# A decoder layer's delta rule: keys and queries turned by VectorE and DRAM, gates by Silu, and another column order

## The chip, the cores and the metric

One core of one Trainium2 chip runs the whole layer in one launch. The time is the device time of one execution in microseconds.

## What is computed

```python
h = x + 0.5 * swiglu(rmsnorm(x), w_in1, w_out1)
h = h + hybrid_mixer(rmsnorm(h))
h = h + 0.5 * swiglu(rmsnorm(h), w_in2, w_out2)
y = rmsnorm(h)

# hybrid_mixer(u), 512 tokens of 1024 channels
hq, hf, hi, hg, gq, gk, gv, ga, gb, gz, gate_h, gate_g = split(u @ w_in)
# branch 1 (HGRN2, 8 heads): forget gates from hf, q = silu(hq), values hi,
#   chunked recurrence, rmsnorm, times silu(hg), projection
# branch 2 (gated delta rule, 8 key heads, 16 value heads)
q, k, v = split(silu(causal_short_conv([gq, gk, gv], conv_w)))   # 4 taps
q, k = l2norm(q) * 128 ** -0.5, l2norm(k)
beta, g = sigmoid(gb), -exp(a_log) * softplus(ga + dt_bias)
o = gated_delta_chunked(q, k, v, beta, g)     # triangular solve per chunk, state across chunks
y_g = (rmsnorm(o) * silu(gz)) @ w_branch_gdn
y = sigmoid(gate_h) * y_h + sigmoid(gate_g) * y_g
return y @ w_out
```

All inputs and outputs are float32. The wide products are made of three products of rounded halves (`mm3`).

## The kernel before

The first feed-forward block takes the span up to about 360 us, the mixer up to about 1240, the second feed-forward block the rest. The change lies in the mixer.

The mixer works on *columns*: 128 output channels of one wide product, for 512 tokens. A column is 24 products (8 slices of the input by 3) into one of two PSUM tiles of the tag `mm`, and its weights come as two slabs of 256 KB through SP's DMA queue, which ScalarE and VectorE split into a rounded half and a rest (`maker`, L1819 and L1821). The string `DENSE` gives the order in which `choose` looks for the next column: Q and F are HGRN's queries and forget gates, B its values and output gates, D the two small gates of the delta rule, k, q, v its keys, queries and values, y the first branch's projection, z its output gates. Columns that aren't eligible yet are passed over; the merge gates (`tgate`) fill in where nothing else is.

Every step is a Python generator. The class `Desk` is a planner: a step asks for an engine and names a duration, for a buffer (`get`), for an event (`on`) or for a pause (`lag`), and the planner puts all steps in an order on each engine before anything is built. That order is what the engines run; its durations (`A(512)`, `V(512)`, `LAG`, `EASE` = 2.5) only serve to make it.

The delta rule runs in eight *units* of one key head and two value heads. For a unit u:

- `conv` (L1125 to L1147) empties a k, q or v column's PSUM tile on ScalarE (L1125), makes the first tap on ScalarE (L1132), the other three on VectorE (L1135), a tanh on ScalarE (L1138), and a product on VectorE (L1144 for k and q, L1147 for v), since x(1 + tanh(x/2)) is 2 silu(x). The factors of 2 are undone later. Keys and queries stay with channels on the partitions.
- Values are then turned to have tokens on the partitions: `turn` (L1156, VectorE, 32x32 blocks) and `bounce` (L1162, L1167: a store to DRAM and a load in another order).
- `norms` turns keys and queries by TensorE: four transposes into a PSUM tile of the one bank `e` (L1196). ScalarE copies the keys out (L1199) and sums the squares of both per token (L1203). It starts when the unit before has its masked matrix, event `N`.
- `g_n` makes the coefficients from the key sums (L1220 to L1231; GpSimd takes a power, L1223), the products of keys with keys and queries (L1242, `pgq`, two halves in the bank `e`), masks them, and multiplies them with decays (L1257, L1263).
- `g_e` makes the decays on ScalarE: an absolute difference (L1184) and an Exp (L1187) for each of two heads.
- `g_b` sends the masked matrix through DRAM (L1275, L1281), and GpSimd inverts 32x32 blocks (L1293, L1294); `g_inv` completes the inverse on TensorE, and `g_rec` runs the recurrence over four chunks.
- The outputs are normalised on ScalarE (L1486), turned, and multiplied with the z gate (`gated`). The last unit's are turned by TensorE (L1500) and split at once (L1514).

When all columns are done, `closing` multiplies the 16 heads' outputs with the second branch's projection; its first two columns (d = 0, 1) go head by head. HGRN's query columns end in `h_q`, its output gates in `gate`, the z columns in `zgate`: a tanh on ScalarE and a product on VectorE each.

Of the kernel before, what the change touches and what calls it, by code (L numbers as in the profile page):

```python
# [11 lines left out]
AF = mybir.ActivationFunctionType  # L12
ALU = mybir.AluOpType
# [3 lines left out]
P = 128  # L17
T = 512
NT = T // P
D = 1024  # L20
# [3 lines left out]
EPS = 1e-6  # L24
# [7 lines left out]
LEVELS = (1, 2, 4, 8, 16)  # L32

DENSE = (
# [3 lines left out]
)  # L38
MERGE = (None, None, "a", "a", "b", "b", None, None)
WB = 6  # L40
# [11 lines left out]
FRESH = 5  # L52
LAG = dict(raw=3.5, gb=6.5, nb=6, m=7, out=6.5, back=6, turn=6.5)
EASE = 2.5
LANES = {"a": 2, "b": 2, "d": 1, "e": 1}


# [631 lines left out]
def mixer(tc, mp, e):  # L689
    nc = tc.nc  # L690
    pe, act, dve, pool, sp = nc.tensor, nc.scalar, nc.vector, nc.gpsimd, nc.sync
# [9 lines left out]
    def v3(ap, a):  # L701
        return ap.rearrange("p (a b) -> p a b", a=a)
# [165 lines left out]
    def h_q(i, pt, new):  # L868
        tag = ("fs", "ut")[i % 2]
        if new:  # L870
            yield "get", "ta", 1
            yield *A(512), 1
            th = ta("th")
            act.activation(th, pt, AF.Tanh, scale=0.5)
            yield "get", tag, 1
            yield *V(560), 1
            qq = hq[i] = place(tag, "qq", (P, NT, 192), 4)
            dve.scalar_tensor_tensor(qq[:, :, :P], v3(th, NT), 1.0, v3(pt, NT), op0=ALU.add, op1=ALU.mult)
            D.put("mm")
            D.put("ta")  # L880
            D.fire(("Q", i))
            return
        yield "get", "ta", 2
        yield "on", "rbc"
        yield *V(512), 1
        qs = ta("qs")
        dve.tensor_tensor(qs, pt, rbc, op=ALU.mult)
        D.put("mm")
        yield A(512)
        th = ta("th")  # L890
        act.activation(th, qs, AF.Tanh, scale=0.5)
        yield "get", tag, 1
        yield V(512)
        qq = hq[i] = place(tag, "qq", (P, NT, 192), 4)
        dve.scalar_tensor_tensor(qq[:, :, :P], v3(th, NT), 1.0, v3(qs, NT), op0=ALU.add, op1=ALU.mult)
        D.put("ta", 2)
        D.fire(("Q", i))

    def h_f(i, pt, new):
# [33 lines left out]
    def h_head(i):  # L933
# [7 lines left out]
        q4 = qp.rearrange("p (c g b) -> p c g b", c=NT, b=2)  # L941
# [11 lines left out]
        at = place("on", "ah", (P, NT, P), 8)  # L953
# [28 lines left out]
        for li, hh in enumerate((1, 2, 4, 8, 16, 32, 64)):  # L982
# [37 lines left out]
            tag = ("x", "we")[i % 2] if hh == 1 else ("w", "ft")[i % 2] if hh == 2 else "tm"  # L1020
# [11 lines left out]
        fe, v, g = fl, hv_[i // 2], hg_[i // 2]  # L1032
# [9 lines left out]
        kn = place(tag_n, "hkn", (P, NT - 1, P), 4)  # L1042
# [5 lines left out]
        for c in range(NT):  # L1048
# [4 lines left out]
            o = po[:, c * P:(c + 1) * P]  # L1053
# [28 lines left out]
            act.activation(on[:, c], po[:, c * P:(c + 1) * P], AF.Square, accum_out=ss[:, c:c + 1])  # L1082

        yield V(4)
        dve.tensor_scalar(rho, ss, 4.0 / P, 4.0 * EPS * 4.0 * P, op0=ALU.mult, op1=ALU.add)
        yield "lag", EASE
        yield "use", "POOL", 1.2
        pool.tensor_tensor(rho, rho, mhalf[:, :NT], op=ALU.pow)
# [10 lines left out]
        pt = ps("pt")  # L1099
# [20 lines left out]
    def conv(k, i, pt, out, n):  # L1120

        yield "get", "ta", 2
        yield *A(512), 1
        ci = ta("ci", (P, T + 32))[:, :T + 3]
        act.copy(ci[:, 3:], pt)  # L1125
        D.put("mm")
        yield V(4)
        dve.memset(ci[:, :3], 0.0)
        wc = [cs[:, C_CV + 4 * i + j:C_CV + 4 * i + j + 1] for j in range(4)]
        yield A(512)  # L1130
        y = ta("cy")
        act.activation(y, ci[:, :T], AF.Copy, scale=wc[0])  # L1132
        for j in range(1, 4):
            yield V(550)
            dve.scalar_tensor_tensor(y, ci[:, j:j + T], wc[j], y, op0=ALU.mult, op1=ALU.add)  # L1135
        yield A(512)
        th = ci[:, :T]
        act.activation(th, y, AF.Tanh, scale=0.5)  # L1138
        a, b = (v3(th, n), v3(y, n)) if n else (th, y)
        if k[0] in "qk" and k[1] > 3:  # L1140
            yield "on", ("K", k[1] - 4)
        yield V(512)
        if n:
            dve.scalar_tensor_tensor(out, a, 1.0, b, op0=ALU.add, op1=ALU.mult)  # L1144
            D.put("ta", 2)
        else:
            dve.scalar_tensor_tensor(y, a, 1.0, b, op0=ALU.add, op1=ALU.mult)  # L1147
            yield V(512)
            turn(th, y)
            D.put("ta")  # L1150
            yield from bounce(f"vn{i}", th, out, "ta")
        D.fire(k)

    def turn(out, x):

        dve.transpose(out.rearrange("p (f c j) -> p f c j", f=4, c=NT), x.rearrange("p (c i f) -> p f c i", c=NT, f=4))  # L1156

    def bounce(name, x, out, tag=None):

        yield S  # L1160
        scr = dr.tile([P, T], F32, name=name)
        sp.dma_start(scr, x)  # L1162
        yield "lag", LAG["turn"]
        if tag:
            D.put(tag)
        yield S
        sp.dma_start(out.rearrange("p (r a) -> p r a", r=4), scr.rearrange("(r i) (f a) -> (i f) r a", r=4, f=4))  # L1167
        yield "lag", LAG["turn"]

    def g_e(u, st):  # L1170

        yield "on", "decays", *([("at", 2 * u + 1)] if u < 2 else ["more"]), *([("R", u - 4)] if u > 3 else []), \
            *([("E", u - 1)] if u else [])
        for i in range(2):
            hd_ = 2 * u + i
            yield "get", "gb", 1
            yield "use", "ACT", .1
            gb = places["gb"]("gb", (P, NT, P))
            act.dma_start(gb, gtd[hd_:hd_ + 1].rearrange("o (c b) -> o c b", c=NT).to_broadcast([P, NT, P]))
            yield "lag", LAG["gb"]  # L1180
            a = G["at"][u % 4 * 2 + i]
            for c in range(NT):
                yield A(200)
                act.activation(a[:, c], gb[:, c], AF.Abs, bias=gam[:, c, hd_:hd_ + 1], scale=-1.0)  # L1184
            D.put("gb")
            yield A(512)
            act.activation(a, a, AF.Exp, scale=-1.0)  # L1187
        D.fire(("E", u))

    def norms(u, i, kq, kn, sm):  # L1190
        yield "on", ("kq"[i], u)
        yield "get", "e", 1
        yield T_(Patient(.5))
        pt = ps("ptk", "e")
        for c in range(NT):
            pe.transpose(pt[:, c * P:(c + 1) * P], kq[:, c, i], ident)  # L1196
        if i == 0:
            yield A(512)
            act.copy(kn, v3(pt, NT))  # L1199
        for c in range(NT):  # L1200
            yield A(300)
            pc = pt[:, c * P:(c + 1) * P]
            act.activation(pc, pc, AF.Square, accum_out=sm[:, 0, 4 * i + c:4 * i + c + 1])  # L1203
        D.put("e")
        D.fire(("norm", u, i))

    def g_n(u, st):
# [9 lines left out]
        hs = slice(2 * u, 2 * u + 2)  # L1217
        rk = sm[:, 1, 0:4]
        yield V(4)
        dve.tensor_scalar(rk, sm[:, 0, 0:4], 4.0 * EPS, None, op0=ALU.add)  # L1220
# [10 lines left out]
        dve.tensor_scalar(c2, c2, 0.5, None, op0=ALU.mult)  # L1231
        D.fire(("C", u))
        yield "on", ("q", u)
        yield "on", ("qm", 0), ("n2", u % 2)
# [145 lines left out]
    def g_rec(u, st):  # L1380
# [34 lines left out]
        for c in range(NT):  # L1415
# [36 lines left out]
            if c < NT - 1:  # L1452
# [5 lines left out]
                else:  # L1458
                    for i in range(2):
# [12 lines left out]
        dve.tensor_scalar(sm[:, 7, 0:4], sm[:, 0, 4:8], 4.0 * P * EPS, 16.0 * P * EPS * EPS, op0=ALU.mult, op1=ALU.add)  # L1472
        dve.scalar_tensor_tensor(v3(rho, 2), v3(ss, 2), 4.0 / P, sm[:, 7:8, 0:4].to_broadcast([P, 2, 4]),
                                 op0=ALU.mult, op1=ALU.add)
        yield "lag", EASE
        yield "use", "POOL", 1.4
# [79 lines left out]
    def zgate(i, pt):  # L1556

        g = G["gz"][i // 2 % 3].rearrange("p c b -> p (c b)")[:, i % 2 * T:i % 2 * T + T]
        yield *A(512), 1
        act.activation(g, pt, AF.Tanh, scale=0.5)  # L1560
        yield *V(560), 1
        dve.scalar_tensor_tensor(g, g, 1.0, pt, op0=ALU.add, op1=ALU.mult)
        D.put("mm")
        D.fire(("z", i))

# [7 lines left out]

    def gate(key, g, t, o):

        yield "get", "thg", 1
        yield A(300)
        th = places["thg"]("thg", (P, 256))
        act.activation(th, o, AF.Tanh, scale=0.5)
        yield V(256)  # L1580
        dve.scalar_tensor_tensor(g[:, t], th, 1.0, o, op0=ALU.add, op1=ALU.mult)
        D.put("thg")
        D.put("mm")
        if t == 3:
            D.fire(key)
# [465 lines left out]
```

## Time and profile before

| | |
|---|---|
| median of 3 runs | 1600.07 us (1598.64 to 1600.56) |
| profiled execution | 1599.18 us, span 1597.3 us |
| TensorE, VectorE, ScalarE, GpSimd busy | 1582.3, 1140.7, 847.6, 415.9 us |
| DMA | 220.63 MB, 138 GB/s in the mean |
| granted TensorE clock | 0.998 |

Busy time is the union of an engine's instructions; TensorE's instructions overlap, so 99% busy does not mean that the array is at its peak. In the rows below, L190 to L192 are the three products of `mm3`. A row of a group ends with the busy time, the mean duration in ns, and the idle time of the engine just before with what ended it. A row of the timeline begins with the start and the duration in us.

### The profile page before, as it was taken

The page shows a single profiled execution, that of the slowest core. Times are in us where ns is not written, and L with a number is a line of the kernel's source. Part 1 is how long each engine was busy: PE and PEld are TensorE (multiplying, and loading weights), DVE is VectorE, ACT ScalarE, POOL GpSimd, SP SyncE. Part 2 cuts the span into 40 slices and gives each one's busy share as a digit, 9 for nine tenths or more (in the row PEclk, how much of TensorE's full clock was granted, in tenths as well). Part 3 has the DMA queues.
Part 4 walks back from the last instruction along what each step waited for, and adds up shares of the span by engine and source line. Part 5 has one row for each costly group of instructions (what it writes and reads, how often), then busy time and mean ns, then how long its engine had stood idle before and what let it go on. Part 6 is the DMA issues. An engine that isn't in the chain of part 4 may idle for free.

```text
span 1597.3 us, 29111 instructions
## 1 busy us (share of the span) xinstructions
PE 1582.3 (99%) x10552; PEld 1374.3 (86%) x10552; DVE 1140.7 (71%) x2220; ACT 847.6 (53%) x1912; POOL 415.9 (26%) x725
## 2 busy tenths in 40 slices
PE   9999999999999999999999999999999999999997
PEld 8899998888888888888878888888788899999887
DVE  6988785448858769746788988875545788879333
ACT  5756674334434344645766666565324666667222
POOL 0211212000312222065725676700001221121001
PEclk9999999999999999999999999999999999999999
DMA  5776873333213213555345535557543687685333
GB/s 181 173 161 157 178 169 98 117 119 108 79 55 93 61 47 110 147 159 151 114 141 157 164 120 181 180 189 220 167 128 125 148 183 159 157 184 143 93 90 118
DMA packets 141984, 220.63 MB, mean 138 GB/s; under 512 B 22144, under 2 KB 43392, under 8 KB 141840
## 3 DMA queue, kind: packets, MB, share of 16 engines
q1 hardware_dynamic: 124848, 188.14, 38.8%
q0 software_dynamic: 14400, 26.22, 10.6%
q10 hardware_dynamic: 2592, 4.42, 1.0%
q8 instruction: 83, 1.36, 0.4%
q14 instruction: 61, 0.50, 0.1%
HBM read 195.88 MB, written 22.84 MB: 137 GB/s over the span
## 4 chain that ended last, share of the span: by engine, by line
PE 90%; DMA 3%; issue 3%; DVE 1%; ACT 1%; SPq 0%; POOL 0%; POOLq 0%; ACTq 0%; DVEq 0%
PE pmm L190 19%; PE pmm L191 19%; PE pmm L192 19%; PE px L192 6%; PE px L191 6%; PE px L190 6%; PE pnat L190 2%; PE pnat L192 2%; PE pnat L191 2%; DMA wlo<-w1b 1%; DMA wlo<-w1a 1%; PE pgq L1242 1%; PE pog L1450 1%; PE pw L1434 1%; PE pl L1005 1%
## 5 line engine op out<-in xcount | busy, mean ns | idle before, releaser
L190 PE MATMUL pmm<-uh,whi 128*128 128x512 f32 x879 | 360.1, 410 | 1.4 <-ACT ci L1125 1.4
L192 PE MATMUL pmm<-uh,wlo 128*128 128x512 f32 x879 | 342.9, 390 | 0.0
L191 PE MATMUL pmm<-ul,whi 128*128 128x512 f32 x879 | 342.3, 389 | 0.5 <-DVE ul L1606 0.3
L192 PE MATMUL px<-xs,wlo 128*128 128x256 f32 x1008 | 285.8, 284 | 1.2 <-DMA wlo<-w1b 0.5
L191 PE MATMUL px<-xs,whi 128*128 128x256 f32 x1008 | 285.3, 283 | 0.0
L190 PE MATMUL px<-xs,whi 128*128 128x256 f32 x1008 | 285.3, 283 | 0.0
L1819 ACT CAST whi<-raw 128x512 fp32r<-128x512 f32 x226 | 140.1, 621 | 221.0 <-PE pmm L191 185.7
L1821 DVE TENSOR_TENSOR wlo<-raw,whi 128x512 fp32r<-128x512 f32 x226 | 160.6, 712 | 116.2 <-ACT whi L1819 113.9
L192 PEld LDWEIGHTS pmm<-uh,wlo 128*128 128x128 f32 x879 | 165.1, 188 | 35.8
L192 PEld LDWEIGHTS px<-xs,wlo 128*128 128x128 f32 x1008 | 193.5, 192 | 1.9 <-DMA wlo<-w1b 0.7
L190 PEld LDWEIGHTS pmm<-uh,whi 128*128 128x128 f32 x879 | 165.6, 188 | 34.0 <-ACT ci L1125 2.0
L190 PEld LDWEIGHTS px<-xs,whi 128*128 128x128 f32 x1008 | 193.5, 192 | 0.1
L191 PEld LDWEIGHTS px<-xs,whi 128*128 128x128 f32 x1008 | 193.5, 192 | 0.1
L191 PEld LDWEIGHTS pmm<-ul,whi 128*128 128x128 f32 x879 | 165.7, 189 | 31.0 <-DVE ul L1606 0.6
L330 ACT CAST whi<-sw 128x512 fp32r<-128x512 f32 x144 | 87.6, 613 | 92.8 <-DVE sw L367 72.9
L309 DVE TENSOR_TENSOR wlo<-raw,whi 128x512 fp32r<-128x512 f32 x100 | 77.7, 788 | 76.6 <-ACT whi L330 76.2
L330 ACT CAST whi<-raw 128x512 fp32r<-128x512 f32 x104 | 61.4, 592 | 127.2 <-PE pmm L191 92.0
L228 POOL TENSOR_TENSOR acc<-acc,sqt 128x512 f32<-128x512 f32 x18 | 23.4, 1301 | 310.6 <-ACT sqt L226 310.6
L309 DVE TENSOR_TENSOR wlo<-sw,whi 128x512 fp32r<-128x512 f32 x144 | 98.1, 682 | 0.0
L330 ACT CAST whi<-rw 128x512 fp32r<-128x512 f32 (+1 forms) x130 | 79.6, 613 | 26.1 <-PE px L191 14.0
L190 PE MATMUL pmm<-xs,whi 128*128 128x512 f32 (+1 forms) x238 | 89.8, 377 | 0.0
L191 PE MATMUL pmm<-xs,whi 128*128 128x512 f32 (+1 forms) x238 | 89.8, 377 | 0.0
(480 smaller groups left out, 3211.5 us busy)
## 6 DMA issues: line engine op xcount, KB each, us to landing
raw<-wt SPq DMA_DIRECT2D x160, 256.0 KB
rw<-w1b SPq DMA_DIRECT2D x80, 256.0 KB
rw<-w1a SPq DMA_DIRECT2D x74, 256.0 KB
wlo<-w1b POOLq DMA_DIRECT2D x53, 256.0 KB, 4.9
wlo<-w1a POOLq DMA_DIRECT2D x47, 256.0 KB, 4.9
raw<-w2b SPq DMA_DIRECT2D x41, 256.0 KB
raw<-w2a SPq DMA_DIRECT2D x36, 256.0 KB
raw<-wn SPq DMA_DIRECT2D x32, 256.0 KB
```

The source lines that it names most:

```text
L190: pe.matmul(pt, ah, bh, start=first, stop=False)
L191: pe.matmul(pt, ah, bl, start=False, stop=False)
L192: pe.matmul(pt, al, bh, start=False, stop=last)
L228: add.tensor_tensor(acc, acc, s, op=ALU.add)
L309: dve.tensor_tensor(lo, x, hi.bitcast(F32), op=ALU.subtract)
L330: act.copy(hi, x)
L1005: pe.matmul(pl_[s0:s0 + 32, c * 16:(c + 1) * 16], ke[:, c * P + s0:c * P + s0 + 32], qv[:, c, r, :, 1], start=True, stop=True)
L1242: pe.matmul(pq[:, (c % 2) * 256:(c % 2) * 256 + 256], kq[:, c, 0], kq[:, c].rearrange("p a b -> p (a b)"), start=True, stop=True)
L1434: pe.matmul(pw[:, hd2[i]], ut[:, 4 * i + c], xs[i], start=True, stop=True)
L1450: pe.matmul(po[:, 256 + i * P:256 + (i + 1) * P], at[i][:, c], w[:, hd2[i]], start=True, stop=True)
L1819: act.copy(hi, raw)
L1821: dve.tensor_tensor(lo, raw, hi.bitcast(F32), op=ALU.subtract)
```

## The change

1. `norms` turns keys and queries as the values are turned: `turn` on VectorE, a store to DRAM and a load (`bounce`). ScalarE then copies the keys and sums the squares from SBUF. Four transposes on TensorE and the PSUM tile go, for each key and each query column.
2. Silu is one operation on ScalarE in `conv`, `h_q`, `gate` and `zgate`, in place of tanh and a product on VectorE; the factors of 2 and 4 in the norms' constants go with it.
3. The first conv tap is on VectorE.
4. In `g_e` the two Exps of a unit stand side by side, booked at 4.0 us.
5. `DENSE` has another order.

```diff
 DENSE = (
-    "F0 Q0 F1 Q1 F2 Q2 F3 Q3 D0 B0 B1 F4 Q4 F5 Q5 B2 F6 Q6 F7 Q7 B3 "
-    "k0 q0 k1 q1 y0 y1 y2 y3 v0 v1 y4 y5 y6 y7 k2 q2 v2 v3 z0 z1 k3 q3 v4 v5 z2 z3 k4 q4 v6 v7 z4 z5 "
-    "k5 q5 v8 v9 z6 z7 k6 q6 v10 v11 z8 z9 k7 q7 v12 v13 z10 z11 v14 v15 z12 z13 z14 z15 "
+    "F0 Q0 Q1 F1 F2 Q2 F3 Q3 D0 B0 F4 B1 Q4 Q5 B2 F5 F6 Q6 F7 Q7 B3 k0 q0 k1 q1 y0 y1 y2 y3 v0 v1 y4 y5 "
+    "y6 y7 k2 q2 v2 v3 k3 v4 q3 z0 z1 v5 q4 k4 z2 z3 v6 v7 z4 z5 v8 k5 q5 v9 z6 k6 q6 z7 v10 v11 z8 k7 "
+    "z9 v12 q7 z10 z11 v13 v14 z12 z13 z14 z15 v15 "
 )
...
+TURNED = (0, 1)
...
     def h_q(i, pt, new):
...
-            th = ta("th")
-            act.activation(th, pt, AF.Tanh, scale=0.5)
...
-            dve.scalar_tensor_tensor(qq[:, :, :P], v3(th, NT), 1.0, v3(pt, NT), op0=ALU.add, op1=ALU.mult)
+            act.activation(qq[:, :, :P], v3(pt, NT), AF.Silu)
...
     def conv(k, i, pt, out, n):
...
-        yield A(512)
+        yield V(512)
         y = ta("cy")
-        act.activation(y, ci[:, :T], AF.Copy, scale=wc[0])
+        dve.tensor_scalar(y, ci[:, :T], wc[0], None, op0=ALU.mult)
...
-        yield A(512)
-        th = ci[:, :T]
-        act.activation(th, y, AF.Tanh, scale=0.5)
...
-        yield V(512)
+        yield A(512)
         if n:
-            dve.scalar_tensor_tensor(out, a, 1.0, b, op0=ALU.add, op1=ALU.mult)
+            act.activation(out, v3(y, n), AF.Silu)
             D.put("ta", 2)
         else:
-            dve.scalar_tensor_tensor(y, a, 1.0, b, op0=ALU.add, op1=ALU.mult)
+            act.activation(y, y, AF.Silu)
...
     def g_e(u, st):
...
-            yield A(512)
+        yield "use", "ACT", 4.0
+        for i in range(2):
+            a = G["at"][u % 4 * 2 + i]
             act.activation(a, a, AF.Exp, scale=-1.0)
...
     def norms(u, i, kq, kn, sm):
         yield "on", ("kq"[i], u)
+        if i in TURNED:
+            yield "get", "ta", 1
+            yield V(900)
+            x = ta("kt")
+            turn(x, kq[:, :, i])
+            yield from bounce(f"{'kq'[i]}n{u}", x, x)
+            x4 = x.rearrange("p (r c j) -> p c r j", r=4, c=NT)
+            if i == 0:
+                yield A(512)
+                act.copy(kn.rearrange("p c (r j) -> p c r j", r=4), x4)
+                D.fire(("kc", u))
+            for c in range(NT):
+                yield A(300)
+                act.activation(x4[:, c], x4[:, c], AF.Square, accum_out=sm[:, 0, 4 * i + c:4 * i + c + 1])
+            D.put("ta")
+            D.fire(("norm", u, i))
+            return
         yield "get", "e", 1
...
     def zgate(i, pt):
...
-        act.activation(g, pt, AF.Tanh, scale=0.5)
-        yield *V(560), 1
-        dve.scalar_tensor_tensor(g, g, 1.0, pt, op0=ALU.add, op1=ALU.mult)
+        act.activation(g, pt, AF.Silu)
...
     def gate(key, g, t, o):
...
-        act.activation(th, o, AF.Tanh, scale=0.5)
-        yield V(256)
-        dve.scalar_tensor_tensor(g[:, t], th, 1.0, o, op0=ALU.add, op1=ALU.mult)
-        D.put("thg")
+        act.activation(g[:, t], o, AF.Silu)
```

More of the change, by code (lines that the diff above doesn't have):

```diff
@@ L870, in h_q @@
         if new:
-            yield "get", "ta", 1
+            yield "get", tag, 1
             yield *A(512), 1
-            th = ta("th")
-            act.activation(th, pt, AF.Tanh, scale=0.5)
-            yield "get", tag, 1
-            yield *V(560), 1
             qq = hq[i] = place(tag, "qq", (P, NT, 192), 4)
-            dve.scalar_tensor_tensor(qq[:, :, :P], v3(th, NT), 1.0, v3(pt, NT), op0=ALU.add, op1=ALU.mult)
+            act.activation(qq[:, :, :P], v3(pt, NT), AF.Silu)
             D.put("mm")
-            D.put("ta")
             D.fire(("Q", i))
             return
-        yield "get", "ta", 2
+        yield "get", "ta", 1
         yield "on", "rbc"
@@ L888, in h_q @@
         D.put("mm")
+        yield "get", tag, 1
         yield A(512)
-        th = ta("th")
-        act.activation(th, qs, AF.Tanh, scale=0.5)
-        yield "get", tag, 1
-        yield V(512)
         qq = hq[i] = place(tag, "qq", (P, NT, 192), 4)
-        dve.scalar_tensor_tensor(qq[:, :, :P], v3(th, NT), 1.0, v3(qs, NT), op0=ALU.add, op1=ALU.mult)
-        D.put("ta", 2)
+        act.activation(qq[:, :, :P], v3(qs, NT), AF.Silu)
+        D.put("ta")
         D.fire(("Q", i))
@@ L1084, in h_head @@
         yield V(4)
-        dve.tensor_scalar(rho, ss, 4.0 / P, 4.0 * EPS * 4.0 * P, op0=ALU.mult, op1=ALU.add)
+        dve.tensor_scalar(rho, ss, 1.0 / P, EPS * P, op0=ALU.mult, op1=ALU.add)
         yield "lag", EASE
@@ L1135, in conv @@
             dve.scalar_tensor_tensor(y, ci[:, j:j + T], wc[j], y, op0=ALU.mult, op1=ALU.add)
-        yield A(512)
-        th = ci[:, :T]
-        act.activation(th, y, AF.Tanh, scale=0.5)
-        a, b = (v3(th, n), v3(y, n)) if n else (th, y)
         if k[0] in "qk" and k[1] > 3:
             yield "on", ("K", k[1] - 4)
-        yield V(512)
+        yield A(512)
         if n:
-            dve.scalar_tensor_tensor(out, a, 1.0, b, op0=ALU.add, op1=ALU.mult)
+            act.activation(out, v3(y, n), AF.Silu)
             D.put("ta", 2)
         else:
-            dve.scalar_tensor_tensor(y, a, 1.0, b, op0=ALU.add, op1=ALU.mult)
+            act.activation(y, y, AF.Silu)
             yield V(512)
+            th = ci[:, :T]
             turn(th, y)
@@ L1154, in turn @@
     def turn(out, x):
-        dve.transpose(out.rearrange("p (f c j) -> p f c j", f=4, c=NT), x.rearrange("p (c i f) -> p f c i", c=NT, f=4))
+        dve.transpose(out.rearrange("p (f c j) -> p f c j", f=4, c=NT), v3(x, NT).rearrange("p c (i f) -> p f c i", f=4) if len(x.shape) < 3 else
+                      x.rearrange("p c (i f) -> p f c i", f=4))
     def bounce(name, x, out, tag=None):
@@ L1191, in norms @@
         yield "on", ("kq"[i], u)
+        if i in TURNED:
+            yield "get", "ta", 1
+            yield V(900)
[10 more added lines that the diff above has]
+                act.activation(x4[:, c], x4[:, c], AF.Square, accum_out=sm[:, 0, 4 * i + c:4 * i + c + 1])
+            D.put("ta")
+            D.fire(("norm", u, i))
+            return
         yield "get", "e", 1
@@ L1219, in g_n @@
         yield V(4)
-        dve.tensor_scalar(rk, sm[:, 0, 0:4], 4.0 * EPS, None, op0=ALU.add)
+        dve.tensor_scalar(rk, sm[:, 0, 0:4], EPS, None, op0=ALU.add)
         yield "lag", EASE
@@ L1230, in g_n @@
         dve.tensor_tensor(c1, c3, eg[:, :, hs], op=ALU.mult)
-        dve.tensor_scalar(c2, c2, 0.5, None, op0=ALU.mult)
         D.fire(("C", u))
@@ L1471, in g_rec @@
         yield "use", "DVE", .4
-        dve.tensor_scalar(sm[:, 7, 0:4], sm[:, 0, 4:8], 4.0 * P * EPS, 16.0 * P * EPS * EPS, op0=ALU.mult, op1=ALU.add)
-        dve.scalar_tensor_tensor(v3(rho, 2), v3(ss, 2), 4.0 / P, sm[:, 7:8, 0:4].to_broadcast([P, 2, 4]),
+        dve.tensor_scalar(sm[:, 7, 0:4], sm[:, 0, 4:8], P * EPS, P * EPS * EPS, op0=ALU.mult, op1=ALU.add)
+        dve.scalar_tensor_tensor(v3(rho, 2), v3(ss, 2), 1.0 / P, sm[:, 7:8, 0:4].to_broadcast([P, 2, 4]),
                                  op0=ALU.mult, op1=ALU.add)
@@ L1559, in zgate @@
         yield *A(512), 1
-        act.activation(g, pt, AF.Tanh, scale=0.5)
-        yield *V(560), 1
-        dve.scalar_tensor_tensor(g, g, 1.0, pt, op0=ALU.add, op1=ALU.mult)
+        act.activation(g, pt, AF.Silu)
         D.put("mm")
@@ L1574, in gate @@
     def gate(key, g, t, o):
-        yield "get", "thg", 1
         yield A(300)
-        th = places["thg"]("thg", (P, 256))
-        act.activation(th, o, AF.Tanh, scale=0.5)
-        yield V(256)
-        dve.scalar_tensor_tensor(g[:, t], th, 1.0, o, op0=ALU.add, op1=ALU.mult)
-        D.put("thg")
+        act.activation(g[:, t], o, AF.Silu)
         D.put("mm")
```

## The prediction

> **What bounds the kernel now.** I read the page's busy times and its chain first.
>
> ```profile
> span 1597.3 us, 29111 instructions
> ...
> PE 1582.3 (99%) x10552; PEld 1374.3 (86%) x10552; DVE 1140.7 (71%) x2220; ACT 847.6 (53%) x1912; POOL 415.9 (26%) x725
> ...
> PE 90%; DMA 3%; issue 3%; DVE 1%; ACT 1%; SPq 0%; POOL 0%; POOLq 0%; ACTq 0%; DVEq 0%
> ```
>
> TensorE is busy for 1582.3 of 1597.3 us and makes 90% of the chain that ended last. So an edit saves time only if it takes instructions off TensorE or removes a wait of TensorE, and it costs time only if TensorE has to wait. The profiled execution took 1599.18 us: 1.9 more than its span and 0.9 less than the median of 1600.07. I sum against 1599.18 and add 0.9 at the end.
>
> Next, TensorE's waits that lie in the mixer (from the list of waits), and the busy times by stretch; the mixer's head loop, delta rule and branch products lie from 364 to 1124 us.
>
> ```profile
> PE pmm L190 <- ACT ci L1125: 1.4, 1, 1.4
> ...
> PE pgq L1242 <- ACT ptk L1203: 0.6, 1, 0.6
> ...
> PE pmm L191 <- DVE ul L1514: 0.2, 1, 0.2
> ```
>
> ```profile
> 800.00:900.00 100.00, 98.55 (x629) 80.66 (x628) 87.52 (x187) 67.41 (x192) 53.11 (x112) 1.00 0.49 149
> ...
> 364.00:1124.00 760.00, 756.35 (x5387) 624.19 (x5385) 584.36 (x1313) 417.67 (x1130) 287.25 (x582) 1.00 0.43 131
> ```
>
> In 760 us TensorE is idle for 3.65. The first wait is for ScalarE to empty a column's PSUM tile, the second for ScalarE's squares of the turned keys and queries, the third for the last head's output. VectorE is busy for 87.5 of 100 us in the delta rule, ScalarE for 67.4. Neither is the bound, but VectorE has the smaller margin. The granted clock is 1.00 throughout.
>
> **Part 1: what TensorE loses.** Sixteen sets (keys and queries of eight units) of four transposes go.
>
> ```profile
> L1196 PE MATMUL ptk<-sq,h 128*128 128x128 f32 x48 | 7.3, 274 | 0.0
> ...
> L1196 PE MATMUL ptk<-sq,x 128*128 128x128 f32 x16 | 2.5, 280 | 0.0
> ```
>
> ```profile
> 673.10 0.60 PE L1196 MATMUL ptk<-sq,h 128*128 128x128 f32 x4
> 673.45 0.48 PE L190 MATMUL pmm<-oh,whi 128*128 128x512 f32 x1
> 673.77 0.40 PE L191 MATMUL pmm<-oh,whi 128*128 128x512 f32 x1
> 674.00 0.40 PE L192 MATMUL pmm<-oh,wlo 128*128 128x512 f32 x1
> ```
>
> The groups show 48 + 16 transposes with 9.8 us of busy time, but busy times of neighbours overlap. What counts is the step from start to start. In the timeline a set holds TensorE from 673.10 to 673.45, that is 0.35 us, and the next product takes 0.32 to its successor where the one after takes 0.23: another 0.09 for the change of kind. A set costs 0.35 us where other short products already stand beside it (they make the change of kind anyway) and 0.44 where it stands alone: 5.6 to 7.0 us for sixteen. Most stand alone, so I take **6.8**. The pgq wait of 0.6 goes too, because the bank it waits for no longer holds turned keys: **0.6**. It could be replaced by another wait of that size, so its bounds are 0 and 0.6.
>
> A rule speaks against this part: the Trainium skill's page "VectorE: DVE Perf Modes", section "Rules for kernel authors", advises TensorE for a 128x128 transpose whose destination may be PSUM, and a crossbar DMA otherwise. By that rule the transposes would stay and 6.8 us would not be saved. The trace speaks against the rule here only in that TensorE is the full engine; no run shows the alternative.
>
> **Part 2: what the other engines get.** On VectorE come sixteen turns and 32 first taps; the product after each gate's tanh goes.
>
> ```profile
> L1156 DVE STREAM_TRANSPOSE ci<-cy 128x512 f32<-128x512 f32 x16 | 17.5, 1096 | 0.2
> ...
> L1144 DVE SCALAR_TENSOR_TENSOR h<-ci,cy 128x512 f32<-128x512 f32 x12 | 8.8, 732 | 1.6 <-ACT ci L1138 1.5
> ...
> L1562 DVE SCALAR_TENSOR_TENSOR ggz<-ggz,pmm 128x512 f32<-128x512 f32 x12 | 8.1, 678 | 0.0
> ...
> L922 DVE TENSOR_SCALAR ke<-fs,cf 128x512 f32<-128x512 f32 x8 | 4.9, 615 | 0.1
> ```
>
> Added: 16 x 1.10 + 32 x 0.62 = 37.4 us. Removed: 32 conv products at 0.73, 16 z and 8 query products at 0.68, and 16 half-size ones that I bound by 0.34 to 0.68: 23.4 + 16.3 + 5.4 to 10.9 = 45 to 51. VectorE gains 8 to 13 us in all, but not in the delta rule: if 26 of the 32 conv columns fall there, it gets the 16 turns (17.6) and 26 taps (16.1) and loses 26 conv products (19.0) and 16 z products (10.8), so its load stays within 4 us of what it is. Off TensorE's path: zero, as long as its order holds.
>
> ScalarE loses 32 taps and gets changes of its function table, since Silu and Exp alternate.
>
> ```profile
> L1132 ACT ACTIVATE cy<-ci,cs 128x512 f32<-128x512 f32 x32 | 22.9, 720 | 7.7 <-DVE ci L1128 5.0 <-issue 1.8 <-ACT ci L1125 0.6
> ...
> L1187 ACT ACTIVATE gat<-gat 128x512 f32<-128x512 f32 x8 | 5.1, 632 | 0.2
> ...
> L1579 ACT ACT_TABLE_LOAD x1 | 1.3, 1283 | 0.0
> L482 ACT ACT_TABLE_LOAD x1 | 1.3, 1283 | 0.0
> ```
>
> ```profile
> 357.38 0.62 ACT L563 ACTIVATE rbc<-h 128x512 f32<-128x512 f32 x1
> 358.02 1.28 ACT L736 ACT_TABLE_LOAD   x1
> ```
>
> Between the load at L1579 (tanh) and that at L482 (Silu, second FFN) no load stands, though Exp, tanh and squares alternate: those share a table, Silu is in another. With both Exps of a unit side by side, each of eight units costs two loads: 16 x 1.28 = 20.5 us, against 32 x 0.72 = 23.0 for the taps. ScalarE's sum is unchanged. What is new is a block of 2 x 1.28 + 2 x 0.63 = 3.8 us; the planner books 4.0. Behind it are queued the eviction of a finished column and the weights' casts. A column is 24 products of 0.23 us, 5.5 us, and there are two PSUM tiles, so a block of 3.8 still fits. Cost taken: zero; bounds: the ci wait of 1.4 gone, or one more of it per unit, 8 x 1.4 = 11. I take 0.7 of gain, half of that wait, since the tap that stood between on ScalarE leaves it.
>
> Whether tanh, which the forget gates and merge gates keep, is in Silu's table too no row shows; L1579's load for tanh comes after Ln, not Silu. If it isn't, some 25 tanh among the Silus cost up to 50 more loads. The planner books none, so I take the shared table and keep the other as a rival.
>
> **Part 3: the keys' new way.** The same trip is made today by the values:
>
> ```profile
> 669.61 1.09 DVE L1156 STREAM_TRANSPOSE ci<-cy 128x512 f32<-128x512 f32 x1
> ...
> 670.73 0.34 SPq L1162 DMA_DIRECT2D vn<-ci  x1
> ...
> 678.67 0.43 SPq L1167 DMA_DIRECT2D gvb<-vn  x1
> ...
> 686.79 0.69 DVE L1301 TENSOR_TENSOR gvb<-gvb,sm 128x512 f32<-128x512 f32 x1 [2.71 <-DMA gvb<-vn]
> ```
>
> From the turn's start to the first use, which did wait for the DMA, are 17.2 us, where the transposes cost under one. Each unit's chain (key norm, coefficients, key product pgq, masked matrix, trip through DRAM, GpSimd's inversion) is that much longer, once per unit, and a unit's norms start only when the unit before has its masked matrix. SP gets 32 issues at about 0.4 us (12.8 us over 400), in order with the weights' loads. What does the longer chain delay?
>
> ```profile
> 821.61 0.16 DVE L1220 TENSOR_SCALAR sm<-sm 128x4 f32<-128x4 f32 x1
> 836.88 1.02 PE L1242 MATMUL pgq<-h 128*128 128x256 f32 x4
> 848.45 1.62 DVE L1257 SCALAR_TENSOR_TENSOR gn<-gm,sm,gat 128x128 f32<-128x128 f32 x4
> 855.09 0.76 DVE L1263 TENSOR_TENSOR gat<-gqm,gat 128x512 f32<-128x512 f32 x1
> ...
> 860.37 0.20 POOL L1294 TENSOR_TENSOR gft<-gft,fm 128x8 f32<-128x8 f32 x1
> 873.75 0.25 POOL L1293 TENSOR_TENSOR fm<-gfs,gln 128x31 f32<-128x31 f32 x1 [7.22 <-DMA gln<-hmask]
> ```
>
> ```profile
> L1294 POOL TENSOR_TENSOR gln<-gln,fm x155: 203/327/875, 725.8 to 1036.0; 128x60 f32<-128x60 f32 x15, 128x28 f32<-128x28 f32 x10, 128x54 f32<-128x54 f32 x10, 128x48 f32<-128x48 f32 x10
> ```
>
> For unit 4 the key sums are ready at 821.61 and pgq starts only at 836.88, because the query's transposes and squares sit in the one bank that pgq needs. That delay of 15.3 us disappears. The sums now come some 16.5 us later, at 838; coefficients take about 7 by the planner's figures (two pauses of 2.5, 1.2, 0.8), so pgq is at 845, its two halves take about 6 in a free bank, and the masked matrix starts at 851 instead of 848.45. GpSimd's inversions run from 725.8 to 1036.0 for seven units, 44.3 us each, with 13 us of waiting before unit 4's. A unit's front part in the new way is 17.2 + 2.6 (copy, squares) + 7 + 6 + 7.4 (848.45 to 855.85) = 40 us: under 44.3, so it doesn't become the cadence. Each unit starts 5 us earlier to 3 later.
>
> The end of the delta rule:
>
> ```profile
> 1111.87 0.40 ACT L1486 ACTIVATE on<-x,sm 128x128 f32<-128x128 f32 x1
> ...
> 1116.77 0.60 PE L1500 MATMUL pto<-sq,on 128*128 128x128 f32 x4
> ...
> 1123.39 0.69 DVE L1514 TENSOR_TENSOR ul<-on,uh 128x512 fp32r<-128x512 f32 x1 [0.74 <-ACT uh L1512]
> ```
>
> TensorE just meets the last head today (a wait of 0.2 on L1514). The outputs were ready at 1112.27 and their transposes stood behind columns until 1116.77: 4.5 us of slack. If TensorE arrives 8.1 us earlier and the last head at the same time, 3.6 us of it are waited out. With a last head that is 5 earlier nothing is, with one 3 later 6.6. I take **2.0**. The new column order is not priced: it moves k3 up by two columns of 5.5 us, k4, k6 and k7 by one, and k5 back by one, which on the whole helps these chains.
>
> **Sum.** 1599.2 - 6.8 - 0.6 - 0.7 + 2.0 = 1593.1; with 0.9, **1594.0**. Own range 1589 to 1598. A measurement of this kernel can tell about 0.2% (3.2 us) from no change.
>
> **Rivals.**
> - *The last head eats it* (0.14). The last head comes 3 to 5 us later, and TensorE waits 6 to 8 us before the last products: 1598 to 1600. For it: today's coincidence at 1123. Against: the 4.5 us of slack.
> - *The DRAM trip becomes the cadence* (0.19), the slower side. If the front part takes more than 44.3 us, as with the present 11.6 from pgq to the mask step instead of 6 (45.6), or with SP's queue holding each DMA for a further 2, the excess adds up over the last five units. At 47 us: 5 x 2.7 = 13.5 late, less 4.5 of slack, on top of the saving that is waited out too: 1599.2 + 13.5 - 4.5 + 0.9 = 1609.
> - *ScalarE's block stops the evictions* (0.05). If ScalarE lost as much again at each switch as the load takes, a unit's block would be 3.8 + 2.6 = 6.4 us, 0.9 over the 5.5 of a column: 8 x 0.9 = 7 us of waits, 1601. Against it, the load at 358.02 starts 0.02 after the end of the instruction ahead. The Trainium skill's "ScalarE: Activation LUTs", section "What ACT_TABLE_LOAD costs", states such a loss: 1283 ns for the load and about 1380 for a drain. The trace agrees on the first and shows no drain.
> - *Tanh is not in Silu's table* (0.05): 50 loads, 64 us more on ScalarE; at one column's wait in four, 12 x 1.4 = 17 us: 1610.
>
> **Numbers.** The forecast has 0.57, of which 0.02 are within 0.2%; the first rival 0.14, of which 0.02 are faster; the second 0.19; the third 0.05, within 0.2%; the fourth 0.05. Faster 0.57, same 0.02 + 0.12 + 0.05 = 0.19, slower 0.24. The range 1587 to 1606 leaves out the worst of the slower cases, and below it only what a better column order might add to 8.1 us.
>
> **What would show it.** Right: no ptk rows on TensorE, 64 fewer short products in 364 to 1124, that stretch some 6 us shorter, 16 to 20 table loads of 1.28 us, inversions still about 44 us apart. Wrong: TensorE waits on L1514 or on ci of several us, GpSimd's inversions 46 us apart or more, over 40 table loads.

## The result, and the profile after

| | before | after |
|---|---|---|
| median, 6 runs each on one chip | 1599.65 us | 1619.2 us (1615.88 to 1623.83) |
| ratio, 95% interval | | 1.0127 [1.0113, 1.0142] |
| profiled execution, span | 1599.18, 1597.3 us | 1617.28, 1615.5 us |
| DMA | 220.63 MB | 229.01 MB |

The change costs about 20 us where 6 less were forecast. The page of the kernel after:

```profile
span 1615.5 us, 28996 instructions
...
PE 1583.6 (98%) x10488; PEld 1370.2 (85%) x10488; DVE 1128.5 (70%) x2188; ACT 846.5 (52%) x1899; POOL 407.9 (25%) x725
...
PE 81%; DMA 7%; issue 5%; DVE 4%; ACT 2%; POOL 0%; SPq 0%; POOLq 0%; DVEq 0%; ACTq 0%
```

TensorE has its 64 transposes fewer (10488 for 10552), and VectorE, ScalarE and GpSimd are all less busy than before. Yet TensorE's busy time rose by 1.3 us, and its share of the chain that ended last fell from 90 to 81%; DMAs have 7% of it instead of 3. So nothing was loaded more: something waits. (The chain's shares don't show that by themselves: `pe_turn` below has 83% for TensorE and 6% for DMAs and loses nothing.) The list of TensorE's waits in the mixer (us in total, times, longest) and the busy times of stretches:

```profile
PE pks L1430 <- DVE s L1466: 4.9, 1, 4.9
PE pog L1457 <- DVE ci L1121: 4.0, 1, 4.0
PE pw L1443 <- DVE x L1434: 1.6, 1, 1.6
PE pmm L191 <- ACT ci L1118: 1.6, 2, 0.9
PE pmm L191 <- ACT uh L1521: 1.5, 1, 1.5
PE pmm L191 <- ACT yh L1577: 1.5, 1, 1.5
```

```profile
364.00:1142.00 778.00, 757.62 (x5335) 620.85 (x5334) 572.54 (x1281) 418.70 (x1120) 278.96 (x582) 0.99 0.45 139
...
880.00:888.00 8.00, 6.93 (x33) 5.44 (x31) 1.48 (x6) 4.58 (x15) 2.04 (x8) 1.00 0.99 284
...
835.20:839.20 4.00, 4.00 (x13) 3.33 (x14) 2.85 (x5) 1.88 (x12) 0.00 (x0) 0.57 0.86 261
...
892.00:897.00 5.00, 5.00 (x13) 3.92 (x14) 3.78 (x8) 1.40 (x4) 4.31 (x9) 0.52 0.69 218
897.00:910.00 13.00, 13.00 (x67) 11.04 (x66) 9.20 (x23) 8.37 (x30) 8.33 (x19) 1.00 0.54 160
```

The mixer's stretch is 18 us longer, and TensorE is idle in it for 20.4 us instead of 3.65. The two longest waits are for VectorE, in the recurrence (for `pog` the row names L1121, the last that VectorE had done; what `pog` reads is `gwe`, which VectorE made just before). What held VectorE is in its groups (line, form, count, busy time, mean ns, idle time before and what ended it):

```profile
L1125 DVE TENSOR_SCALAR cy<-ci,cs 128x512 f32<-128x512 f32 x32 | 15.6, 487 | 26.4 <-DMA vn<-ci 13.0 <-DMA od<-zo 6.2 <-DMA td<-tg 3.7
```

The first tap, now on VectorE, is cheap (0.487 us), but five of the 32 wait 22.9 us in all for *stores*: of turned values (`vn<-ci`), of gated outputs (`od<-zo`), of a merge gate (`td<-tg`). The tap reads none of these. It writes `cy`, a buffer of the tag `ta`, and that buffer was last read by the store. The chain that ended last shows one case link by link:

```profile
880.17 7.71 DMA od<-zo
887.98 0.49 DVE cy L1125
...
890.74 0.75 DVE cy L1128
891.88 1.22 PE pks L1430 x2
```

A store issued at 880.17 lands at 887.9, in a stretch with the DMA engines at 0.99; only then the tap has its buffer. Behind it on VectorE stands the copy of the state (L1466) that TensorE's `pks` needs, so TensorE stops for 4.9 us. The 4.0 us wait at 835 has the same history: VectorE's tap stood for 5.64 us until a store of turned values, issued at 823.64, had landed at 829.43. After both waits the clock is low: in 892 to 897 it is 0.52, against 1.00 from 897 on, and in the 4 us after 835 it is 0.57. The products of those 5 us are about 0.43 us apart instead of 0.23, some 2 us more for each long wait. A third such stretch lies at the mixer's end (a clock of 0.50 in 1143 to 1145, after waits of 1.0 and 1.5 us). That is most of why busy time rose with fewer instructions. The Trainium skill's "TensorE: Matmul & The Clock Gate", section "Part 1: The HAM clock gate (the 'warmup' mystery)", says that TensorE falls to half rate after an idle window of about 3.4 us. For the two long waits the trace agrees; the runs also show half rate after less. In `slots8` below, products slow to 0.43 us apart from 709.8 on (clock 0.50 in 710 to 712) after a wait of 1.4 us that ended at 708.26, and not after the wait of 2.1 us that ended at 881.99.

The tag has six buffers. Before, its tiles were held for a column's taps or for a store. Now a turned key's or query's buffer `kt` is held from the turn through both DMAs and the squares. The third unit in the timeline, whose key was turned at 687.84:

```profile
688.98 0.38 SPq L1153 DMA_DIRECT2D kn<-kt  x1
...
697.92 0.42 SPq L1158 DMA_DIRECT2D kt<-kn  x1
...
706.12 0.62 ACT L1194 COPY gkn<-kt 128x512 f32<-128x512 f32 x1 [4.05 <-DMA kt<-kn]
```

From the store's issue to the first use are 17.1 us, and ScalarE stands 4.05 us for the load. From the turn's start it is 18.3 us, the longest of the eight units; the others take 15.2 to 17.7. The buffer is free only after the last square, so it is held longer still. When the tap stands from 881.7 to 887.9, two of the six buffers hold the sixth unit's key and query:

```profile
868.51 1.08 DVE L1146 STREAM_TRANSPOSE kt<-h 128x512 f32<-128x512 f32 x1
...
872.28 1.10 DVE L1146 STREAM_TRANSPOSE kt<-h 128x512 f32<-128x512 f32 x1
...
879.64 0.59 ACT L1118 COPY ci<-pmm 128x512 f32<-128x512 f32 x1
...
880.91 0.58 ACT L1118 COPY ci<-pmm 128x512 f32<-128x512 f32 x1
...
900.98 0.29 ACT L1198 ACTIVATE kt<-kt 128x128 f32<-128x128 f32 x1
```

The last of their squares runs at 900.98. Two buffers hold columns that were just emptied (`ci`), one the turned values whose store was issued at 881.39, and one the gated output whose store lands at 887.9. That makes six.

### The profile page after: what moved, and what is told of

Read it like the earlier page. It is cut to its first block, busy times and chain, and to the rows that moved or that the text cites. A ratio compares the mean times of both kernels' runs of the same rounds, so it can differ in the third digit from the quotient of the medians.

```text
span 1615.5 us, 28996 instructions
## 1 busy us (share of the span) xinstructions
PE 1583.6 (98%) x10488; PEld 1370.2 (85%) x10488; DVE 1128.5 (70%) x2188; ACT 846.5 (52%) x1899; POOL 407.9 (25%) x725
## 2 busy tenths in 40 slices
DMA packets 152735, 229.01 MB, mean 142 GB/s; under 512 B 22656, under 2 KB 52096, under 8 KB 152592
## 4 chain that ended last, share of the span: by engine, by line
PE 81%; DMA 7%; issue 5%; DVE 4%; ACT 2%; POOL 0%; SPq 0%; POOLq 0%; DVEq 0%; ACTq 0%
PE pmm L191 18%; PE pmm L192 17%; PE pmm L193 17%; PE px L193 5%; PE px L192 5%; PE px L191 5%; DMA wlo<-w1b 2%; DMA wlo<-w1a 2%; PE pnat L191 2%; PE pnat L193 2%; PE pnat L192 2%; DMA vn<-ci 1%; PE pgq L1251 1%; PE pog L1459 1%; PE pw L1443 1%
## 5 line engine op out<-in xcount | busy, mean ns | idle before, releaser
L191 PE MATMUL pmm<-uh,whi 128*128 128x512 f32 x879 | 363.8, 414 | 4.7 <-ACT uh L1521 1.5
```

The source lines that it names most:

```text
L191: pe.matmul(pt, ah, bh, start=first, stop=False)
```

## The experiments

Main theory (S): the longer trip holds buffers of `ta`, the taps wait for them, and TensorE behind the taps. Its rivals: Silu's table loads on ScalarE (T); the new plan with its column order (O). For what is left behind S: the wait for the trip, whose DMAs are booked at 6.5 us each and slower on the chip (L); the longer key chain, which delays the last heads (D); the trip's traffic and SP's issues; other waits of the plan (P). All kernels were timed against the kernel before. In `slots8`, `tap_scalar`, `no_trip`, `trip_unused` and `kt_apart` the planner's bookings are untouched, so the order of the steps stays; the others are planned anew, which turned out to matter.

**More buffers, the same order.** The planner goes on counting six, the chip has eight; the tile `ci` gets smaller so that they fit.

```diff
-TA = 6
+TA = 8
-    D = Desk(... ta=TA, ...
+    D = Desk(... ta=6, ...
-        ci = ta("ci", (P, T + 32))[:, :T + 3]
+        ci = ta("ci", (P, T + 4))[:, :T + 3]
```

> The changed kernel with eight instead of six physical buffers of the tag ta; the planner still counts six, so every engine has the same instructions in the same order and only the buffer addresses differ. Theory S (the first tap, now on VectorE, waits at the head of VectorE's queue for a buffer that a store to DRAM still reads; five such waits of 22.9 us in all, and TensorE then waits 11.6 us and runs some microseconds at a lower rate): these waits go, about 1603. Rival T (table loads on ScalarE) and rival O (the new plan and column order): within 2 us of the changed kernel's 1619.

Measured: 1605.06 us, 1.0041 [1.0026, 1.0056], 14.1 below the kernel after. The tap's line (its idle time until), then TensorE's longest wait and the stretch:

```profile
its engine sat idle before it (us, times) until:
  ACT ci L1118: 1.7, 2
```

```profile
PE pks L1430 <- DVE s L1466: 2.1, 1, 2.1
```

```profile
364.00:1130.00 766.00, 754.26 (x5328) 618.65 (x5328) 574.34 (x1282) 417.98 (x1119) 282.62 (x582) 1.00 0.45 140
```

All waits of the tap for stores are gone, TensorE's idle time falls from 20.4 to 11.7, and its busy time by 3.4: the low clock at 835 and at 892 is gone, and one short stretch at 710 has come. S is confirmed for 14 of the 20 us; T and O had forecast no gain.

**The tap on ScalarE.** Is it the tap's new place in VectorE's queue that costs? The first tap goes back to ScalarE at the same place of the order.

```diff
-        dve.tensor_scalar(y, ci[:, :T], wc[0], None, op0=ALU.mult)
+        act.activation(y, ci[:, :T], AF.Copy, scale=wc[0])
```

> The changed kernel with the first tap issued on ScalarE again, at the place in the plan where it stands now, so TensorE's, GpSimd's and SP's orders are unchanged. Theory S: the five buffer waits move from VectorE's queue to ScalarE's, which holds up evictions and casts instead; about half of the loss returns, 1605 to 1612. Rival T: no gain or 2 us worse, since ScalarE gets 23 us more. Rival O: within 2 us of 1619.

Measured: 1620.29 us, 1.0128 [1.0106, 1.0150]. No gain, though S had let me expect 7 to 14 us; the time alone is what T and O said. The same waits stand at the same line, on ScalarE:

```profile
its engine sat idle before it (us, times) until:
  DMA vn<-ci: 11.4, 3
  DMA od<-zo: 6.4, 1
  DMA td<-tg: 4.5, 1
```

So the tap's place is not what costs: whichever engine asks for the buffer stands, and holding up ScalarE cost as much as holding up VectorE. T and O don't fall by this run but by the one before and the next.

**Transposes back on TensorE, all else changed.**

```diff
-TURNED = (0, 1)
+TURNED = ()
```

> The changed kernel with keys and queries turned by TensorE again (TURNED empty); Silu, tap and column order stay, and the planner makes a new plan. Theory S (the DRAM trip holds ta buffers for some 17 us each and so makes the buffer waits): few waits of the first tap on DMAs; 6.8 us of transposes come back; 1600 to 1606. Rival T: 1619 or more, since all table loads stay. Rival O: 1612 to 1620.

Measured: 1598.52 us, 0.9993 [0.9983, 1.0002], not told from the kernel before, and a little under the range of S. Its stretch and its longest wait:

```profile
364.00:1124.00 760.00, 758.34 (x5395) 624.90 (x5395) 560.70 (x1265) 421.50 (x1120) 291.46 (x582) 1.00 0.43 131
```

```profile
PE pq L1355 <- ACT acc L1348: 0.6, 1, 0.6
```

Silu with its table loads, the first tap on VectorE and the new order together cost nothing, so T and O are out. The turn, with the plan that it brings, makes the difference: 1619.2 - 1598.5 = 20.7 us.

**The order of columns.** The kernel after with the old `DENSE`, and the kernel before with the new one alone.

```diff
 DENSE = (
-    "F0 Q0 Q1 F1 F2 Q2 F3 Q3 D0 B0 F4 B1 ...
+    "F0 Q0 F1 Q1 F2 Q2 F3 Q3 D0 B0 B1 F4 ...
```

> The changed kernel with the column order of before; the planner makes a new plan. Theory S: the waits of the first tap stay in kind, 1611 to 1620. Rival O (the column order is what costs): about 1600. Rival T: 1615 to 1620.

> The kernel before with the new column order alone; a new plan, nothing else changed. If the new order is good in itself: 1590 to 1598. If it only suits the other edits: 1602 to 1625. The changed kernel with the old order took 1647.

Measured: 1647.35 us, 1.03 [1.0283, 1.0317], and 1615.37 us, 1.0092 [1.0069, 1.0114]. No theory had 1647; 1615 is the second case of its expectation. Swapped between the two kernels, the orders cost 28 and 16 us; yet the new order loses nothing in `pe_turn`, so an order needn't be made for a kernel to suit it. The order is part of the change, and a kernel that is planned anew can have a loss of this size in it whatever else it shows.

**Three kernels planned anew.** The first books 8 us instead of 6.5 for each DMA of a trip, on top of `slots8`; the second also lets the planner count eight buffers; the third is `slots8` with only the queries going through DRAM. The edits of the first two, then of the third:

```diff
-LAG = dict(..., turn=6.5)
+LAG = dict(..., turn=8)
...
-TURNED = (0, 1)
+TURNED = (1,)
```

> Eight physical buffers of ta as in the run with eight, and the planner books 8 us instead of 6.5 for each of the two DMAs of a trip through DRAM (keys, queries, values, outputs); the planner makes a new plan. Theory L (what is left of the loss comes from the trip being longer than booked: ScalarE stands at the head of its queue for the turned keys' DMA, 9 us in three waits): these waits go, 1597 to 1601. Rival D (the longer key chain delays the last heads, whatever is booked): 1603 to 1610, with the waits before the last products.

> Eight buffers of ta, of which the planner knows too, and 8 us booked for each DMA of a trip; a new plan. Theory L: 1596 to 1600. Rival D: 1603 to 1610. If the planner's freedom to use two more buffers makes buffer waits again, the first tap waits for DMAs on VectorE and the time is 1605 or more.

> Eight physical buffers; only the queries go through DRAM, the keys are turned by TensorE, so 32 of the 64 transposes stay; a new plan. Rival D (the key chain is what costs): 1598.5 less 3.4 of saved transposes, 1595. Theory L: ScalarE's wait for the keys' DMA goes too, but the queries' squares may wait as much: 1595 to 1600. If the trip costs by its DMAs and SP issues alone: half of the loss, about 1602.

Measured: 1620.26 us, 1.0120 [1.0093, 1.0148]; 1606.56 us, 1.0039 [1.0028, 1.0051]; 1610.99 us, 1.0064 [1.0042, 1.0086]. L's expected gain didn't come. `ta8_lag8` lies in D's range and has 6.1 us of waits at the last head (L1509, L1521), and none of a tap for a store; the other two lie in no range. These runs decide little: their TensorE waits are at other places than the kernel after's. `slots8_lag8` has its most, 8.7 us in four, on the eviction of columns (L1118), `ta8_lag8` 3.1 on the last head's outputs (L1509), `q_slots8` 7.0 on L1118 again. By the two kernels above, a new plan on an old order can do that alone.

**The trip itself, the same order.** From `slots8`, once without the two DMAs of keys and queries, and once with both, the load going to a DRAM buffer that nobody reads. Both leave out the second half of the keys' and queries' turning, so their results are wrong.

```diff
-        sp.dma_start(scr, x)
+        name[0] in "kq" or sp.dma_start(scr, x)
...
-        sp.dma_start(out.rearrange("p (r a) -> p r a", r=4), ...
+        name[0] in "kq" or sp.dma_start(out.rearrange("p (r a) -> p r a", r=4), ...
```

```diff
-        sp.dma_start(out.rearrange("p (r a) -> p r a", r=4), ...
+        sp.dma_start(dr.tile([P, T], F32, name=name + "u").rearrange("p (r a) -> p r a", r=4) if name[0] in "kq" else out.rearrange("p (r a) -> p r a", r=4), ...
```

> The changed kernel with eight physical buffers, without the store and the load of the turned keys and queries (32 DMAs); ScalarE copies and squares what the turn on VectorE left, so keys, norms and output are wrong; every engine's instructions keep their order but for the DMAs left out. Theory L (the rest of the loss is waiting for the trip): 1605 falls to the 1598.5 of the kernel with TensorE's transposes less their 6.8 us, 1592, and no wait on kt's DMA is left. Rival P (the plan's other waits, which the turns on VectorE and the squares from SBUF brought): 1602 to 1606.

> As the run without the trip, but both DMAs of each trip are issued at their places: the store, and a load of the same shape that goes to another buffer in DRAM, for which nobody waits. The traffic and SP's issues are there, only the wait for the load is gone (the squares in place still wait for the store). Theory L with the wait as its cause: 1592, as without the trip. If SP's queue and the DMA traffic are what delays the rest: 1603 to 1606.

Measured: 1598.97 us, 1.0004 [0.9994, 1.0013], and 1601.38 us, 1.0011 [1.0000, 1.0021]. Both lie between the figures that L (1592) and its rivals (1602 or 1603 to 1606) gave. The 32 stores and loads with their issues on SP make 2.4 us by the medians (1598.97 to 1601.38) and 1.1 by the ratios, with intervals that overlap: not told from nothing. Waiting for the load makes another 3.7 (1601.38 to 1605.06), 4.8 by the ratios, with intervals apart. Where that wait stands, `slots8` shows in ScalarE's waits, at the copy of the keys:

```profile
ACT gkn L1194 <- DMA kt<-kn: 7.5, 2, 4.7
```

Without any trip, and with no transposes on TensorE, the kernel is still not faster than before. Its stretch and TensorE's waits say why:

```profile
364.00:1124.00 760.00, 751.93 (x5328) 617.18 (x5328) 573.80 (x1281) 418.01 (x1119) 284.36 (x582) 1.00 0.42 131
```

```profile
PE pmm L191 <- ACT ci L1118: 1.6, 2, 0.9
PE pmm L191 <- ACT uh L1521: 1.5, 1, 1.5
PE pmm L191 <- ACT yh L1577: 1.5, 1, 1.5
PE pmm L192 <- DVE ul L1608: 1.2, 2, 1.0
PE pmm L191 <- ACT ggz L1569: 1.0, 1, 1.0
PE pmm L191 <- ACT tg L1557: 0.7, 1, 0.7
```

TensorE is busy for 751.93 us where `pe_turn` has 758.34, 6.4 us less, and idle for 8.07 where `pe_turn` has 1.66. (Both stretches last 760 us, so the 6.4 more is the same figure; what it shows is that the same work ends no earlier.) The transposes are saved, and the plan gives the time back: 4.8 us at columns that ScalarE evicts late (`ci`, `yh`, `ggz`, `tg`) and 2.9 at the mixer's end (L1608, L1521, L1523). Why the plan puts those evictions late (the planner counts six buffers, of which the trip holds more) is argued from the code and was not isolated.

**Keys and queries in buffers of their own.** Six buffers again, and two more for `kt` alone, with the order of the kernel after and the smaller tile `ci` of `slots8`.

```diff
-    ... t64:2 on:2"),
+    ... t64:2 on:2 kt:2"),
...
-            x = ta("kt")
+            x = places["kt"]("kt")
```

> The changed kernel with two buffers of their own for the turned keys and queries, outside ta, which stays at six; the planner counts as before, so all engines have the same instructions in the same order. If the turned keys' hold of ta buffers (17 us and more each) is what makes the first taps wait: 1605, as with eight buffers, and no wait of a first tap on a DMA. If the values' and outputs' stores alone make the waits: 1615 to 1620.

Measured: 1609.31 us, 1.0054 [1.0039, 1.0069]. In the tap's line:

```profile
its engine sat idle before it (us, times) until:
  ACT ci L1118: 1.7, 2
```

Again no tap waits for a store, with the same six buffers for everything else. It is the turned keys and queries in `ta` that make those waits. The time, between the two that were expected, lies 4 us above `slots8`, by intervals that overlap.

**A version made for it.** `slots8` with 8 us booked (`turn=8`), and an order of columns searched for these bookings with the kernel's own planner.

```diff
 DENSE = (
+    "Q0 F0 F2 Q1 Q3 Q2 F4 F1 B0 F3 D0 Q4 B1 Q5 B2 Q6 F6 F7 k0 Q7 F5 B3 q0 k1 q1 y0 y1 v0 y2 v1 k2 y4 "
+    "y5 y3 y7 q2 y6 z0 k3 v3 v2 z1 v4 v5 q3 q4 k4 z3 v6 z5 v7 z4 z2 v8 k5 q5 z6 v9 q6 k6 v10 z7 z8 v11 "
+    "k7 z9 v12 q7 z10 z15 z11 v13 v15 z13 z14 v14 z12 "
```

> Eight physical buffers, 8 us booked for each DMA of a trip, and a column order searched for this plan (the other plan with 8 us booked had no such order and took 1620). If buffers, the booked trip and the order are all that stands between the saved transposes and the time: 1594 to 1599, under both kernels or level with before. If the trip costs in other ways: 1602 or more.

Measured: 1597.23 us (1595.92 to 1598.46, ten runs), 0.9983 [0.9974, 0.9993]. The stretch, and the longest waits that are left:

```profile
364.00:1124.00 760.00, 754.05 (x5340) 619.67 (x5339) 576.93 (x1284) 422.02 (x1122) 284.72 (x582) 1.00 0.46 142
```

```profile
PE pmm L191 <- ACT uh L1521: 1.5, 1, 1.5
PE pmm L192 <- DVE ul L1608: 1.3, 2, 1.0
PE pmm L191 <- ACT yh L1577: 1.0, 1, 1.0
```

With the buffers, the booking and the order, the same turn through DRAM is 22 us faster than the kernel after and 0.17% under the kernel before, at the limit of what can be measured here. From `pe_turn` (0.9993 [0.9983, 1.0002]) it isn't told apart, and for that kernel no order was searched. Idle time is 5.95 us, half of it at the mixer's end (L1608, L1521). Which of booking and order did it isn't shown: `slots8` with an order of its own and 6.5 us booked was not run.

## Why the prediction was wrong

The way from `pe_turn` to the kernel after, in medians; the second and third terms are from the two stretches and are one figure with two signs:

| | us |
|---|---|
| `pe_turn` | 1598.5 |
| transposes leave TensorE | -6.4 |
| waits in the plan without any trip | +6.4 |
| stores and loads, their issues and traffic | +2.4 |
| waiting for the load | +3.7 |
| waiting for buffers of `ta`, with the low clock after | +14.1 |
| sum (medians: 1619.2) | 1618.7 |

- *Part 1, what TensorE loses: right.* 6.4 us less busy against 6.8 taken. The pgq wait went as well. The rule of the Trainium skill's "VectorE: DVE Perf Modes", section "Rules for kernel authors", that keeps 128x128 transposes on TensorE, set aside there, came out right for this kernel: `pe_turn` is 20.7 us faster. The size of that is this plan's: the way through DRAM in `lag8_order` isn't told apart from `pe_turn`.
- *Part 2, ScalarE: right.* The groups of the kernel after have eight table loads at the Exps and 24 in all; tanh comes without loads of its own, so the rival of the missing table is out. The block is as short as booked, with no drain in it:

```profile
646.61 1.28 ACT L1175 ACTIVATE gat<-gb,gx 128x128 f32<-128x128 f32 x4
647.91 1.28 ACT L1180 ACT_TABLE_LOAD   x1
649.20 1.15 ACT L1180 ACTIVATE gat<-gat 128x512 f32<-128x512 f32 x2
```

  The load starts 0.02 us after the work before it and the Exps 0.01 after the load, so the second loss that the Trainium skill's "ScalarE: Activation LUTs", section "What ACT_TABLE_LOAD costs", states does not show here. `pe_turn` carries the block and loses nothing, so the third rival is out too. The 0.7 of gain did not come in the kernel after: its waits on L1118 are 1.6.
- *Part 2, VectorE: the load right, "off TensorE's path: zero, as long as its order holds" wrong.* The load fell, a tap takes 0.487 and not 0.62. But I asked only how long VectorE works and not what its new instruction needs before it can start: a buffer.
- *Part 3: the failed step.* It asked "what does the longer chain delay?" and followed units, inversions and the last head. The 17.2 us from turn to first use were right (15.2 to 18.3). It never counted what is *held* for those 17 us and until the squares are done: one of six buffers, for each of 16 trips. The prediction does not mention `ta`, though the diff shows `get "ta"` ahead of the turn and `put` behind the squares. The term for the waits was 2.0. The one wait that it priced, for the last head, has that size: 1.8 us at L1521 and L1523, where the kernel before has 0.2. All waits together are 6.4 + 2.4 + 3.7 + 14.1 = 26.6; waiting for buffers, 14.1 of them, was put at nothing without a reason.
- *SP's 32 issues* were put at 0.4 us each and hidden. They and the traffic make 2.4 by the medians, not told from nothing.
- *"The new column order is not priced"* hid a term as large as the result: 28 us between the two orders in the kernel after. As the change comes with its order the sum was not wrong by it, but it was luck that nothing hung on it.
- *The rivals.* "The DRAM trip becomes the cadence" has the right sign and comes nearest, 1609 against 1619.2, but not by its mechanism. GpSimd's inversions from the first to the last, in the kernel after and in `pe_turn`:

```profile
L1303 POOL TENSOR_TENSOR gln<-gln,fm x155: 204/315/856, 705.4 to 1064.7; 128x60 f32<-128x60 f32 x15, 128x28 f32<-128x28 f32 x10, 128x54 f32<-128x54 f32 x10, 128x48 f32<-128x48 f32 x10
```

```profile
L1303 POOL TENSOR_TENSOR gln<-gln,fm x155: 203/322/897, 705.7 to 1040.2; 128x60 f32<-128x60 f32 x15, 128x28 f32<-128x28 f32 x10, 128x54 f32<-128x54 f32 x10, 128x48 f32<-128x48 f32 x10
```

  Over seven units that is 51.3 and 47.8 us each. `pe_turn` passes the sign I had set, 46 apart, and loses nothing; so inversions this far apart cost nothing by themselves, and 44.3 was no limit. The last head did not eat it either: TensorE waits for it 1.8 us, not 6 to 8, and the long waits lie at 835 and 892, in the recurrence. The other signs of being wrong did not appear either: waits for the eviction to ci are 1.6 us in the kernel after (1.4 before), and table loads are 24, not over 40.

## What to carry to other kernels

When a step becomes longer, count what it holds meanwhile, not only what waits for its result: list the buffers between its `get` and its `put`, multiply by the new duration, and ask which instruction needs the next buffer and what stands behind it on its engine. An instruction that waits for a store whose data it never reads is, as here, waiting for a buffer; two more buffers with the order unchanged is the cheapest test. With a planned order, isolate a cause only with edits that leave the plan alone: a new plan on an order made for another kernel cost 16 and 28 us here, and nothing in a third case.

## What was not expected of the hardware

A wait of TensorE of 4 to 5 us costs more than itself: the granted clock was 0.57 over the next 4 us and 0.52 over the next 5, and product steps 0.43 instead of 0.23 us, about 2 us each, which is about the size of the 3.4 us of busy time that `slots8` took back. Nor is a long wait needed: after one of 1.4 us `slots8` shows about 3.4 us at half rate. And a store of 256 KB (`od<-zo`) took 7.7 us from issue to landing with the DMA engines at 0.99, where the planner books 6.5.
